# First RMSNorm of a diffusion trunk: squares summed onto all partitions by a matrix of ones, root on ScalarE, reciprocal on VectorE

## The chip, the cores and the metric

The kernel runs on one NeuronCore of a Trainium2 chip. The metric is the device time of one execution in microseconds (us). The engines are TensorE (PE; its weight loads are listed apart as PEld), VectorE (DVE), ScalarE (ACT), GpSimd (POOL) and SyncE (SP), which issues nearly all DMAs. Each engine works through its own instructions in order and waits for the others by semaphores.

## The reference, cut to what matters

The reference is a trunk of two layers over 256 latent and 256 context tokens of 1024 channels. Each layer starts with an RMSNorm whose result is scaled and shifted by values computed from two conditioning vectors, and multiplies it with one wide projection:

```python
def rmsnorm(x, g):
    xf = x.astype(jnp.float32)
    y = xf * lax.rsqrt(jnp.mean(xf * xf, axis=-1, keepdims=True) + EPS)
    return (y * g.astype(jnp.float32)).astype(x.dtype)
...
def modulate(h, shift, scale):
    return h * (1 + scale) + shift
...
        mod = (s_lat @ w_ada[l] + b_ada[l])[:, None, :]
        sh1, sc1, g1, sh2, sc2, g2 = jnp.split(mod, 6, axis=-1)
...
        h = modulate(rmsnorm(x, norm1_g[l]), sh1, sc1)
        hc = modulate(rmsnorm(xc, norm1_g[l]), csh1, csc1)
        p = h @ w_in[l]
```

All of it is in float32. The rest of a layer (convolution branch, neighbourhood attention, gates, two output projections and a gated MLP) is not touched by the change.

## The kernel before, in words

Channels lie on the 128 partitions and tokens along the free axis. `x` is held as eight tiles of 128 channels by 512 tokens (256 latent, then 256 context). A float32 product is made as three products of rounded parts (`mm3`, L177 to L179; in `v_tile`, L629, the parts are told apart by `parts`): a weight unit of 128x1024 is loaded by SP (`raw`), ACT rounds it to `whi`, DVE takes the rest as `wlo`, and the activations `h` are split in the same way.

The tile framework orders each engine's instructions by a plan of its own; `tc.issue_after` and the helper `queued` (L133) tie some of them to others, and `queued` above all makes one line of the first PE instructions.

The first stage is what the change touches. In order:

- Constants are set (`one`, `mhalf`), ACT loads the table of Silu and makes `sil`, the Silu of the conditioning vectors, when `cv` has come. PE runs 14 products of `ident` with itself (`busy`, L127), which write to a bank that nothing reads.
- The loop over the eight tiles (from L521) loads `x[k]`, squares it on ACT (L525; the context half of the last on DVE, L528), adds two squares on DVE (L532) and sums over the channels on PE (`sum0`, L515): for each block of 128 tokens, the squares are the stationary operand and a column of ones the moving one, so that the sums of 512 tokens come out as four columns of `sums0`, with tokens on the partitions. `busy(3)` follows each of the first three sums. Between them stand the two halves of `ada0` (`ada_half`, L200): products of `sil` with the weights `w_ada` of the scale and shift of channel tile 0.
- `root` (L332): DVE divides by 1024 and adds EPS, POOL raises to -0.5 (L336), and PE transposes the four columns, broadcast to 128 wide, with `ident` (L341), which puts 1/rms of all tokens on all partitions in a bank `po`. ACT copies it to SBUF later (L663).
- Meanwhile `ada_rows` (ACT copy, L217) and `ada_sums` (two PE transposes L224, a DVE reduction L226, the bias L228) make scale and shift of channel tile 0, and `gain` (L285) makes (1 + scale) times the norm's weight.
- `modulated` (L347) makes `h` of channel tile k: DVE multiplies `x` by gain and 1/rms (L355), ACT adds the shift and rounds (L356), DVE keeps the rest (L357).
- The loop over k (L690) then runs the products of V (`v_tile`, L629), a part of the first convolution projection (`glu0`), and, one tile ahead, the scale and shift of tile k + 1 (`ada_now`), whose weights come as two units of 512 KB for each k into four buffers that are used in turn.

From there on PE has work without a break through both layers, up to the last norm.

Of the kernel before, what the change touches and what calls it, by code (L numbers as in the profile page):

```python
# [15 lines left out]
P = 128  # L16
# [29 lines left out]
def trunk(ctx: ExitStack, tc: tile.TileContext, xt, cvec, crow, wall, wada, params, bias_t, rope_t, out):  # L46
# [28 lines left out]
    def sl(w, i):  # L75
        return w[:, i * P : (i + 1) * P]
# [39 lines left out]
    act.activation(small([P, 1], "wb", 4), one, AF.Silu)  # L116
    mhalf = cp.tile([P, 4], F32, name="mhalf")
    dve.memset(mhalf, -0.5)
    sil = ea0.tile([P, 2 * KD + 32], F32, name="sil")
    dve.memset(sil, 0.0)  # L120
    act.activation(sil[:, : 2 * KD], cv.rearrange("p k s -> p (k s)"), AF.Silu)


    warm = psum("sc")
    def busy(n):
        for _ in range(n):
            mm = pe.matmul(sl(warm, 0), ident, ident, start=True, stop=True)  # L127
        return mm


    queue = [busy(14)]

    def queued(f, *a):  # L133
        with tc.issue_after(queue[-1].ins):
            queue.append(f(*a))
# [7 lines left out]
    def raw_unit(src, r=None):  # L143
        r = wp.tile([P, UW], F32, tag="raw", bufs=4, name=nm("raw")) if r is None else r
        lastdma[0] = sp.dma_start(r, src)
        return r
# [51 lines left out]
    def ada_half(ps, u, r):  # L198
        for g in range(4):
            mm = pe.matmul(  # L200
                ps[32 * g : 32 * g + 32, :S], sil[:, 8 * u + 2 * g : 8 * u + 2 * g + 32], r[:, g * S : (g + 1) * S],
                start=u == 0, stop=u == 1,
            )
        return mm

    def ada_products(l, j, bank, place=lambda: None):

        ps = psum(bank)
        for u in range(2):
            ada_half(ps, u, raw_unit(wada[l, 2 * j + u], place()))  # L210
        return ps

    lastev = [None]
# [1 line left out]
    def ada_rows(ps):  # L215
        ev = tmp()[:, :S]
        lastev[0] = act.copy(ev, ps[:, :S])  # L217
        return ev

    def ada_sums(l, j, ev):  # L220
        n = slice(j, j + 9, 8) if l == 0 and j < 8 else slice(2 * j, 2 * j + 2)
        pt = psum("pt")
        for i in range(2):
            mm = pe.transpose(sl(pt, i), sl(ev, i), ident)  # L224
        m = mods[l][:, n, :]
        dve.tensor_reduce(m, pt[:, :S].rearrange("p (i g s) -> p i s g", i=2, g=4)[:, :, 0:2, :], AX.X, ALU.add)  # L226
        b = par[:, l * NPAR + BADA : l * NPAR + BADA + 6 * KD][:, n].unsqueeze(2).to_broadcast([P, 2, 2])
        dve.tensor_tensor(m, m, b, ALU.add)  # L228
        return mm
# [32 lines left out]
                    tmp().bitcast(BF16), r, v, 1.0, pr(l, BADA + n, 1), ALU.mult, ALU.add, mods[l][:, n, s : s + 1]  # L262
                )

    def ada_now(j, place):
        ev = ada_rows(ada_products(0, j, "po", place))
        yield
        ada_sums(0, j, ev)
        gain(0, 1, N1G, j)
# [9 lines left out]
    def gain(l, part, off, k, ns=2):  # L279

        if (l, part) not in gains:
            gains[l, part] = cp.tile([P, KD, 2], F32, name=f"gain{l}_{part}")
        a = gains[l, part][:, k, :ns]
        g = pr(l, off + k, 1).to_broadcast([P, ns])
        dve.scalar_tensor_tensor(a, mod2(l, part, k)[:, :ns], 1.0, g, ALU.add, ALU.mult)  # L285
# [46 lines left out]
    def root(pt, nt, n, bank):  # L332
        red = small([P, nt], "red")
        mid = dve.tensor_scalar(red, pt[:, :nt], 1.0 / n, EPS, ALU.mult, ALU.add)
        rs = small([P, nt], "rs")
        pool.tensor_tensor(rs, red, mhalf[:, :nt], ALU.pow)  # L336
        yield mid
        yield
        pb = psum(bank)
        for t in range(nt):  # L340
            pe.transpose(sl(pb, t), rs[:, t : t + 1].to_broadcast([P, P]), ident)  # L341
        return pb
# [170 lines left out]
    sums0 = psum("pt")  # L513

    def sum0(q, first, last):  # L515
        for t in range(4):
            mm = pe.matmul(sums0[:, t : t + 1], sl(q, t), one, start=first and t == 0, stop=last, skip_group_check=True)
        return mm

    ada0 = psum("po")  # L520
    for k in range(KD):  # L521
        sp.dma_start(x[k], xt[k])
        q = tmp()
        if k < KD - 1:
            act.activation(q, x[k], AF.Square)  # L525
        else:
            act.activation(q[:, LAT], x[k][:, LAT], AF.Square)
            dve.tensor_tensor(q[:, CTX], x[k][:, CTX], x[k][:, CTX], ALU.mult)  # L528
        if k >= KD - 2:
            queued(sum0, q, False, k == KD - 1)  # L530
        elif k % 2:
            dve.tensor_tensor(q, q, prev, ALU.add)  # L532
            queued(sum0, q, k == 1, False)
            queued(busy, 3)
        prev = q
        if k >= KD - 3 and k != KD - 2:
            ra = raw_unit(wada[0, k // (KD - 1)])
            if k < KD - 1:
                queued(ada_half, ada0, 0, ra)
# [3 lines left out]
    for l in range(DEPTH):  # L543
# [5 lines left out]
        with ExitStack() if last else start as e1a:  # L549
# [68 lines left out]
            with ExitStack() as e1b:  # L618
# [4 lines left out]
                def v_tile(pv, w, k, toks, parts=range(3)):  # L623
                    i = k % 2
                    for t in toks:
                        c = slice(t * P, (t + 1) * P)
                        b = slice(i * 512, (i + 1) * 512)
                        for n in parts:
                            pe.matmul(  # L629
                                pv[t], h1[n == 1][k][:, c], w[n == 2][:, b], start=k + n == 0, stop=k == KD - 1 and n == 2  # L630
                            )

                if l == 0:

# [4 lines left out]
                    def place():  # L639
                        places[0] += 1  # L640
                        if places[0] % 2:
                            return eb.tile([P, UW], F32, tag="q", bufs=2, name=nm("raw"))
                        return eb.tile([P, UW], F32, tag="k", bufs=2, name=nm("raw"))

                    sums = root(sums0, 4, D, "po")
                    next(sums)
                    ev = ada_rows(ada0)
                    rv = wp.tile([P, UW], F32, tag="raw", bufs=4, name=nm("raw"))
                    wv = [wp.tile([P, UW], F32R, tag=t, bufs=4, name=nm(t)) for t in ("whi", "wlo")]
# [10 lines left out]

                    def more():
                        act.copy(wg[0][:, cuts[0]], rg[:, cuts[0]])
                        act.copy(pb, ps)  # L663
                        act.copy(wv[0][:, cuts[1]], rv[:, cuts[1]])
                        act.copy(wg[0][:, cuts[1]], rg[:, cuts[1]])
                        for w, r, c in ((wv, rv, cuts[0]), (wg, rg, cuts[0]), (wv, rv, cuts[1])):
                            low_part(w, r, c)

                    queued(busy, 2)
                    queued(ada_sums, 0, 0, ev)  # L670
                    gain(0, 1, N1G, 0)
                    with tc.issue_after(queue[-1].ins):
                        ps = whole(sums)
                        queue.append(busy(6))
                    pb = tp.tile([P, 512], F32, tag="ss", name="rstd0")
                    pg0 = [psum("sc") for _ in range(2)]

                    wgs = {0: wg}
# [11 lines left out]
                    for k in range(KD):  # L690
                        if k % 2 == 0 and k:
                            with tc.issue_after(low[0].ins), tc.issue_after(low[1].ins):
                                wv = wunit(l, U_V + k // 2, cuts=2)
                        low = modulated(0, ps if k == 0 else pb, 1, 0, k, h1, (0, 1))
                        if k == 0:
                            with tc.issue_after(low[0].ins), tc.issue_after(low[1].ins):
                                more()
                            with tc.issue_after(queue[-1].ins):
                                v_tile(pv, wv, k, range(4), parts=(0,))
                            v_tile(pv, wv, k, range(4), parts=(1,))  # L700
                        elif k == 1:
                            with tc.issue_after(low[1].ins):
                                low_part(wg, rg, cuts[1])
                        if k == 5:
                            with tc.issue_after(lastdma[0].ins):
                                sp.dma_start(par[:, DW:], params[:, DW:])
                                sp.dma_start(rope, rope_t)
                        if k + 1 < KD:
                            nxt = ada_now(k + 1, place)
                            next(nxt)  # L710
                        v_tile(pv, wv, k, range(4), parts=range(3) if k else (2,))
                        if k + 1 < KD:
                            finish(nxt)
                        glu0(2 if k else 1)
# [220 lines left out]
        with ExitStack() as e2:  # L935
# [101 lines left out]
                    ffn_out(i - 3, pss[2 * i - 6], pss[2 * i - 5])  # L1037
            if not last:
                h1 = h_tiles()
            if last:  # L1040
                eps = small([P, 1], "wb", 4)
                dve.memset(eps, EPS)
            sss = sum_squares(NS, S, last)
            NB = 0 if last else KD - 2
            if not last:
# [167 lines left out]
```

## Time and profile before

| | us |
|---|---|
| median of 3 runs | 1130.89 |
| lowest and highest run | 1130.51, 1132.48 |
| span of the profiled execution, first to last instruction | 1127.4 |
| PE busy in the span | 1115.5 |
| DVE busy | 906.5 |
| ACT busy | 565.7 |
| first product of the V projection (L629) | at 18.03 |

The profile gives the span of the profiled execution, which is 3.5 us under the median of the timed runs; what lies before its first and after its last instruction is not in it. A line of the profile names the line of the kernel, the engine, the operation, and the tiles as out<-in. In the timeline a line is start, duration, engine, and what was made; in the chain of waits, start and the time that it added to the chain. A float32 product of two operands is recorded as two passes, so that 14 products of `busy` stand as x28. Matmuls overlap, so that one's recorded duration is longer than the time between two of them.

### The profile page before, as it was taken

The page shows a single profiled execution, that of the slowest core. Times are in us where ns is not written, and L with a number is a line of the kernel's source. Part 1 is how long each engine was busy: PE and PEld are TensorE (multiplying, and loading weights), DVE is VectorE, ACT ScalarE, POOL GpSimd, SP SyncE. Part 2 cuts the span into 40 slices and gives each one's busy share as a digit, 9 for nine tenths or more (in the row PEclk, how much of TensorE's full clock was granted, in tenths as well). Part 3 has the DMA queues.
Part 4 walks back from the last instruction along what each step waited for, and adds up shares of the span by engine and source line. Part 5 has one row for each costly group of instructions (what it writes and reads, how often), then busy time and mean ns, then how long its engine had stood idle before and what let it go on. Part 6 is the DMA issues. An engine that isn't in the chain of part 4 may idle for free.

```text
span 1127.4 us, 17780 instructions
## 1 busy us (share of the span) xinstructions
PE 1115.5 (99%) x6854; PEld 965.1 (86%) x6854; DVE 906.5 (80%) x1625; ACT 565.7 (50%) x937; POOL 17.2 (2%) x24
## 2 busy tenths in 40 slices
PE   9999999999999999999999999999999999999997
PEld 7678777787789988888888888989898999999997
DVE  4689999786778788888898555789996898988773
ACT  4347657542334543444334223544677667766642
POOL 0000000000000000000000000010000000000000
PEclk9999999999999999999999999999999999999999
DMA  8832231635734354545556656555533575665781
GB/s 325 310 100 89 92 117 38 200 99 198 248 120 145 110 170 133 184 152 155 165 181 205 214 188 197 176 194 174 154 109 120 180 247 175 187 193 182 213 274 57
DMA packets 53941, 190.83 MB, mean 169 GB/s; under 512 B 6240, under 2 KB 6496, under 8 KB 53856
## 3 DMA queue, kind: packets, MB, share of 16 engines
q1 hardware_dynamic: 53568, 189.65, 52.6%
q8 instruction: 54, 0.88, 0.3%
q14 instruction: 31, 0.25, 0.1%
q10 hardware_dynamic: 288, 0.04, 0.0%
HBM read 188.62 MB, written 1.05 MB: 168 GB/s over the span
## 4 chain that ended last, share of the span: by engine, by line
PE 85%; DVE 10%; DMA 2%; ACT 2%; issue 1%; POOL 0%; SPq 0%; DVEq 0%; ACTq 0%; POOLq 0%
PE main L177 25%; PE main L179 24%; PE main L178 24%; DVE cb L576 4%; PE main L629 4%; DVE wlo L159 2%; DMA raw<-in_wall 1%; PE sc L127 1%; PE sc L177 1%; PE sc L179 1%; PE sc L178 1%; PE po L200 1%; PE po L502 1%; DMA sb<-in_crow 1%; PE sc L430 0%
## 5 line engine op out<-in xcount | busy, mean ns | idle before, releaser
L177 PE MATMUL main<-h,whi 128*128 128x256 f32 (+1 forms) x1328 | 446.8, 337 | 0.0
L179 PE MATMUL main<-h,wlo 128*128 128x256 f32 (+1 forms) x1328 | 443.4, 335 | 0.5 <-DVE wlo L159 0.5
L178 PE MATMUL main<-h,whi 128*128 128x256 f32 (+1 forms) x1328 | 442.4, 333 | 0.0
L158 ACT CAST whi<-raw 128x1024 fp32r<-128x1024 f32 (+1 forms) x244 | 252.5, 1039 | 284.7 <-PE main L178 128.6
L159 DVE TENSOR_TENSOR wlo<-raw,whi 128x1024 fp32r<-128x1024 f32 (+1 forms) x244 | 293.7, 1209 | 113.3 <-ACT whi L158 108.6
L177 PEld LDWEIGHTS main<-h,whi 128*128 128x128 f32 x1328 | 249.5, 188 | 32.0 <-issue 3.9
L179 PEld LDWEIGHTS main<-h,wlo 128*128 128x128 f32 x1328 | 249.5, 188 | 28.9 <-DVE wlo L159 0.7
L178 PEld LDWEIGHTS main<-h,whi 128*128 128x128 f32 x1328 | 249.9, 188 | 28.1 <-issue 0.2
L576 DVE SCALAR_TENSOR_TENSOR cb<-u,par,cb 128x512 f32<-128x512 f32 (+1 forms) x240 | 140.6, 620 | 1.2
L261 DVE CUSTOM_DVE_ANT_0 t<-raw,sb,par 128x1024 bf16<-128x1024 f32 x100 | 126.9, 1280 | 1.4 <-ACT sb L245 1.2
L177 PE MATMUL main<-fh,whi 128*128 128x256 f32 (+1 forms) x386 | 123.0, 319 | 0.0
L178 PE MATMUL main<-fl,whi 128*128 128x256 f32 (+1 forms) x386 | 122.9, 319 | 0.0
L179 PE MATMUL main<-fh,wlo 128*128 128x256 f32 (+1 forms) x386 | 122.9, 318 | 0.0
L178 PEld LDWEIGHTS main<-fl,whi 128*128 128x128 f32 x386 | 72.7, 188 | 5.6
L177 PEld LDWEIGHTS main<-fh,whi 128*128 128x128 f32 x386 | 72.7, 188 | 5.6
L179 PEld LDWEIGHTS main<-fh,wlo 128*128 128x128 f32 x386 | 72.7, 188 | 5.5
L948 ACT ACTIVATE t<-main,par 128x512 f32<-128x512 f32 (+1 forms) x82 | 50.7, 669 | 35.3 <-PE main L179 35.3
L949 DVE SCALAR_TENSOR_TENSOR t<-main,par,t 128x510 f32<-128x510 f32 (+1 forms) x82 | 47.6, 616 | 8.2 <-ACT t L948 7.6
L952 DVE SCALAR_TENSOR_TENSOR t<-main,par,t 128x510 f32<-128x510 f32 (+1 forms) x82 | 46.6, 611 | 0.0
L356 ACT ACTIVATE h<-t,mod 128x256 fp32r<-128x256 f32 x56 | 25.2, 502 | 37.5 <-DVE t L355 37.4
L883 DVE SCALAR_TENSOR_TENSOR x<-main,mod,x 128x256 f32<-128x256 f32 x48 | 22.1, 480 | 23.6 <-PE main L179 23.4
L629 PE MATMUL main<-whi,h 128*128 128x512 f32 x128 | 40.6, 402 | 0.0
(217 smaller groups left out, 1198.0 us busy)
## 6 DMA issues: line engine op xcount, KB each, us to landing
raw<-in_wall SPq DMA_DIRECT2D x239, 512.0 KB, 4.2
raw<-in_wada SPq DMA_DIRECT2D x88, 512.0 KB, 4.4
bias<-in_bias_t SPq DMA_DIRECT2D x8, 640.0 KB, 4.4
row<-in_wada SPq DMA_DIRECT2D x8, 512.0 KB, 4.8
sb<-in_crow SPq DMA_DIRECT2D x5, 512.0 KB, 6.1
x<-in_xt SPq DMA_DIRECT2D x8, 256.0 KB, 4.6
raw<-in_wall SPq DMA_DIRECT2D x8, 256.0 KB, 6.8
out<-t SPq DMA_DIRECT2D x3, 256.0 KB, 2.1
```

What stands on the lines that cost most here:

```text
L158: act.copy(hi[:, c], r[:, c])
L159: dve.tensor_tensor(lo[:, c], r[:, c], hi[:, c].bitcast(F32), ALU.subtract)
L177: pe.matmul(ps, w[0], xh, start=start, stop=False)
L178: pe.matmul(ps, w[0], xl, start=False, stop=False)
L179: pe.matmul(ps, w[1], xh, start=False, stop=stop)
L261: dve.tensor_tensor_reduce(tmp().bitcast(BF16), r, v, 1.0, pr(l, BADA + n, 1), ALU.mult, ALU.add, mods[l][:, n, s : s + 1])
L356: high = act.activation(hi[:, c], y[:, c], AF.Identity, bias=b)
L576: dve.scalar_tensor_tensor(cb[j], src, w, cb[j], ALU.mult, ALU.add)
L629: pe.matmul(pv[t], h1[n == 1][k][:, c], w[n == 2][:, b], start=k + n == 0, stop=k == KD - 1 and n == 2)
L948: act.activation(c, pv_, AF.Identity, bias=pr(l, FDB + t, 1), scale=w[1])
L949: dve.scalar_tensor_tensor(c[:, :, 1:], pv_[:, :, : S - 1], w[0], c[:, :, 1:], ALU.mult, ALU.add)
L952: dve.scalar_tensor_tensor(c[:, :, : S - 1], pv_[:, :, 1:], w[2], c[:, :, : S - 1], ALU.mult, ALU.add)
```

## The change

`sum0` becomes one product for each tile of squares, with a 128x128 matrix of ones as stationary and the 512 squares as moving operand: the sums come out on all partitions at once. ACT takes the root of sums/1024 + EPS (a new use of the Sqrt table, loaded ahead, behind `sil`), DVE the reciprocal, in place in the SBUF tile `pb`. `root` with POOL's power and the four transposes, and ACT's copy of `po`, are gone for this norm. The squares of tiles 1, 3 and 5 go to DVE. The first `busy` has 11 products, the one behind the first sum has 2, those behind the second and third sum are gone. For channel tile 0 the gain is made straight from the reduction, as sum times weight plus (1 + bias) times weight, the second made ahead, so that the bias need not be added first. The first products of `ada_now` are tied behind V's. `EPS` becomes one tile for both uses.

```diff
+    eps = cp.tile([P, 1], F32, name="eps")
+    dve.memset(eps, EPS)
...
+    act.activation(small([P, 1], "wb", 4), one, AF.Sqrt)
...
-    queue = [busy(14)]
+    queue = [busy(11)]
...
-    def ada_products(l, j, bank, place=lambda: None):
+    def ada_products(l, j, bank, place=lambda: None, after=None):
         ps = psum(bank)
         for u in range(2):
-            ada_half(ps, u, raw_unit(wada[l, 2 * j + u], place()))
+            r = raw_unit(wada[l, 2 * j + u], place())
+            with tc.issue_after(after.ins) if after else ExitStack():
+                ada_half(ps, u, r)
...
         m = mods[l][:, n, :]
+        if (l, j) == (0, 0):
+            g, first = pr(0, N1G, 1), small([P, 1], "wb", 4)
+            dve.scalar_tensor_tensor(first, pr(0, BADA + KD, 1), 1.0, g, ALU.add, ALU.mult)
         dve.tensor_reduce(m, pt[:, :S].rearrange("p (i g s) -> p i s g", i=2, g=4)[:, :, 0:2, :], AX.X, ALU.add)
+        if (l, j) == (0, 0):
+            gains[0, 1] = cp.tile([P, KD, 2], F32, name="gain0_1")
+            dve.scalar_tensor_tensor(gains[0, 1][:, 0, :], mod2(0, 1, 0), g, first.to_broadcast([P, 2]), ALU.mult, ALU.add)
...
     def sum0(q, first, last):
-        for t in range(4):
-            mm = pe.matmul(sums0[:, t : t + 1], sl(q, t), one, start=first and t == 0, stop=last, skip_group_check=True)
-        return mm
+        return pe.matmul(sums0, one.to_broadcast([P, P]), q, start=first, stop=last)
...
-        if k < KD - 1:
-            act.activation(q, x[k], AF.Square)
-        else:
+        if k == KD - 1:
             act.activation(q[:, LAT], x[k][:, LAT], AF.Square)
             dve.tensor_tensor(q[:, CTX], x[k][:, CTX], x[k][:, CTX], ALU.mult)
+        elif k % 2:
+            dve.tensor_tensor(q, x[k], x[k], ALU.mult)
+        else:
+            act.activation(q, x[k], AF.Square)
...
             queued(sum0, q, k == 1, False)
-            queued(busy, 3)
+            if k == 1:
+                queued(busy, 2)
...
-                    sums = root(sums0, 4, D, "po")
-                    next(sums)
+                    pb = tp.tile([P, 512], F32, tag="ss", name="rstd0")
+                    act.activation(pb, sums0, AF.Sqrt, bias=eps, scale=1.0 / D)
+                    dve.reciprocal(pb, pb)
...
-                        act.copy(pb, ps)
...
-                    gain(0, 1, N1G, 0)
-                    with tc.issue_after(queue[-1].ins):
-                        ps = whole(sums)
-                        queue.append(busy(6))
-                    pb = tp.tile([P, 512], F32, tag="ss", name="rstd0")
+                    queued(busy, 6)
...
-                        low = modulated(0, ps if k == 0 else pb, 1, 0, k, h1, (0, 1))
+                        low = modulated(0, pb, 1, 0, k, h1, (0, 1))
...
-                            nxt = ada_now(k + 1, place)
+                            nxt = ada_now(k + 1, place, None if k else vmm)
```

The order on the engines that follows from it differs from the old one in the first stage and hardly anywhere else. On SP the second half of V's unit for k = 4 is issued ahead of the `w_ada` units of k = 3, and the rest of the parameters (352 KB) ahead of those of k = 5. On ACT and DVE one rounding and one subtraction for a later weight unit change places with a neighbour, late in that loop.

More of the change, by code (lines that the diff above doesn't have):

```diff
@@ L263, in ada_dots, with ada_now @@
                 )
-    def ada_now(j, place):
-        ev = ada_rows(ada_products(0, j, "po", place))
+    def ada_now(j, place, after):
+        ev = ada_rows(ada_products(0, j, "po", place, after))
         yield
@@ L628, in v_tile @@
                         for n in parts:
-                            pe.matmul(
+                            mm = pe.matmul(
                                 pv[t], h1[n == 1][k][:, c], w[n == 2][:, b], start=k + n == 0, stop=k == KD - 1 and n == 2
                             )
+                    return mm
                 if l == 0:
@@ L699, in trunk @@
                                 v_tile(pv, wv, k, range(4), parts=(0,))
-                            v_tile(pv, wv, k, range(4), parts=(1,))
+                            vmm = v_tile(pv, wv, k, range(4), parts=(1,))
                         elif k == 1:
@@ L1039, in trunk @@
                 h1 = h_tiles()
-            if last:
-                eps = small([P, 1], "wb", 4)
-                dve.memset(eps, EPS)
             sss = sum_squares(NS, S, last)
```

## The prediction

> **What bounds the kernel now.** The page's head first: one engine is never idle.
>
> ```profile
> span 1127.4 us, 17780 instructions
> PE 1115.5 (99%) x6854; PEld 965.1 (86%) x6854; DVE 906.5 (80%) x1625; ACT 565.7 (50%) x937; POOL 17.2 (2%) x24
> ```
>
> PE is busy for 1115.5 us of 1127.4, but the mean says nothing about the stage that changes. So next the busy time by stage: the first 18 us, and the V projection behind them (columns: stretch, its length, then for PE, PEld, DVE, ACT and POOL busy us and instructions, granted clock, DMA share, GB/s).
>
> ```profile
> 18.00:62.00 44.00, 43.98 (x272) 30.75 (x272) 27.47 (x65) 20.29 (x41) 0.00 (x0) 1.00 0.76 275
> ```
>
> Behind 18 us PE has no gap, so whatever lets that stage begin earlier lets it end earlier, as long as the transfers keep up. What sets its beginning is read from the chain of waits (start, time added):
>
> ```profile
> 1.83 5.78 PE sc L127 x28
> ...
> 8.40 0.78 PE sc L127 x6
> ...
> 10.74 0.79 PE pt L517 x8
> 11.53 0.78 PE sc L127 x6
> 12.30 0.57 PE po L200 x8
> 12.87 1.88 PE pt L517 x16
> 14.75 0.57 PE po L200 x8
> 15.31 0.64 PE sc L127 x4
> ...
> 16.76 1.34 PE sc L127 x12
> 18.10 2.05 PE main L629 x8
> 20.15 1.00 PE po L200 x16
> ```
>
> It is PE's own queue: filler products (L127), the sums (L517) and the first conditioning products (L200) stand one behind the other, and the sums over tiles 6 and 7 begin at 12.87 only because the fillers of 11.53 and a conditioning half stand ahead. Had their inputs come by then? The start of ACT and DVE in the timeline:
>
> ```profile
> 1.65 1.28 ACT L116 ACT_TABLE_LOAD   x1 [1.65 <-PEq L1202]
> ...
> 3.82 0.21 ACT L121 ACTIVATE sil<-cv 128x16 f32<-128x16 f32 x1 [0.67 <-DMA cv<-in_cvec]
> ...
> 5.94 2.69 ACT L525 ACTIVATE t<-x 128x512 f32<-128x512 f32 x4 [0.86 <-DMA x<-in_xt]
> ...
> 10.14 0.63 ACT L525 ACTIVATE t<-x 128x512 f32<-128x512 f32 x1 [1.51 <-DMA x<-in_xt]
> ...
> 10.83 0.43 DVE L528 TENSOR_TENSOR t<-x 128x256 f32<-128x256 f32 x1 [1.48 <-DMA x<-in_xt]
> ```
>
> Tile 6 is squared by 10.77 and tile 7 by 11.26: about 2 us of the chain is PE's queue, not data. From the sums to the first V product:
>
> ```profile
> 15.38 0.37 ACT L217 COPY t<-po 128x256 f32<-128x256 f32 x1 [4.15 <-PE po L200]
> ...
> 16.28 0.17 DVE L226 TENSOR_REDUCE mod<-pt 128x4 f32<-128x16 f32 x1 [1.33 <-PE pt L224]
> ...
> 16.69 0.16 DVE L285 SCALAR_TENSOR_TENSOR gain<-mod,par 128x2 f32<-128x2 f32 x1
> 16.95 0.87 DVE L355 SCALAR_TENSOR_TENSOR t<-x,gain,po 128x256 f32<-128x256 f32 x2
> 17.47 0.91 ACT L356 ACTIVATE h<-t,mod 128x256 fp32r<-128x256 f32 x2 [1.20 <-DVE t L355]
> 18.03 2.12 PE L629 MATMUL main<-whi,h 128*128 128x512 f32 x8
> ```
>
> L355 at 16.95 needs the gain (made at 16.69 from the second conditioning half) and 1/rms. The V products follow 1.08 us later. The start of L355 is the quantity to forecast.
>
> **The change part by part.** The prices of the new operations, from the nearest rows: a product with a matrix of ones (chain of waits at the layer norm), ACT from PSUM with pointers and without, DVE by one source and by two, and the reciprocals there are.
>
> ```profile
> 229.19 0.86 PE po L832 x2
> ...
> L948 ACT ACTIVATE t<-main,par 128x512 f32<-128x512 f32 x42 | 30.4, 774 | 35.3 <-PE main L179 35.3
> L591 ACT ACTIVATE t<-main 128x512 f32<-128x512 f32 x3 | 1.8, 597 | 0.0
> ...
> L574 DVE TENSOR_SCALAR cb<-u,par 128x512 f32<-128x512 f32 x4 | 2.2, 546 | 0.0
> L532 DVE TENSOR_TENSOR t<-t,t 128x512 f32<-128x512 f32 x3 | 2.1, 693 | 6.3 <-ACT t L525 6.3
> ...
> L453 DVE RECIPROCAL ri<-sm x32: 151/158/173, 89.4 to 857.8; 128x1 f32<-128x1 f32 x32
> L469 DVE RECIPROCAL ri<-sm x8: 156/159/171, 121.3 to 191.8; 128x2 f32<-128x2 f32 x8
> ```
>
> *Sums.* One costs 0.86 us where four narrow products cost 0.79: five of them lose 0.35 us of PE. In return the fillers lose 3 + 1 + 3 + 3 products.
>
> *Table and squares.* The Sqrt table load stands behind `sil`, at 4.03. As L116 it takes 1.28 and its trial 0.20, so tile 0 is squared at about 5.45 to 6.08, not at 3.95. DVE has squared tile 1 by then (0.69), adds by 6.80, and PE's 11 fillers end there too: 28 passes took 5.78 with the last 6 at 0.13 each, so the slow ones took 0.227, and 1.83 + 22 x 0.227 = 6.82. First sum 6.83 to 7.69, two fillers to 8.14. DVE squares and adds tile 3 by 8.12 (two times 0.69 from 6.72), tile 5 by 9.44. The sums run at 8.17 and 9.50, the second to 10.36.
>
> The Trainium skill ("ScalarE: Activation LUTs", What ACT_TABLE_LOAD costs) charges 2.66 us for every switch of set, 1.28 of load and 1.38 of drain. This trace has the load at 1.28 and no such drain: L116's activation follows at 2.95.
>
> *Tail.* Conditioning half 0 (0.57) from 10.36 to 10.93; its weights were issued ahead of tile 6, which ACT took at 10.14. Sums of tiles 6 and 7: 10.93 + 2 x 0.86 = 12.65. Half 1 then runs from 12.65 to 13.29 (recorded 0.64 from its start). Its weights came at 5.2 + 6.8 = 12.0:
>
> ```profile
> L145 SPq DMA_DIRECT2D raw<-in_wada x1: 708/708/708, 5.2 to 5.2; - x1
> ...
> DMA to landing us min/median/max: 6.8/6.8/6.8
> ```
>
> *Root.* The last pass ends at 12.81. Sqrt from PSUM with one pointer lies between 0.60 (L591) and 0.77 (L948); I take 0.69, ending 13.54. ACT's copy of the conditioning rows waits behind it, at about 13.45 instead of 15.38: 1.93 earlier, and the transposes and the reduction L226 with it, at 14.35. `more` loses one ACT copy, and POOL's power and four transposes go; none of that was the last to arrive, so I count nothing.
>
> *Reciprocal.* It runs from 13.58 and delays nothing until it takes more than 0.77, when it holds up L226 on DVE's queue. No trace row is wider than two elements. From below it is the 0.55 of L574. From above the rows bound it badly: the medians grow by 1 ns for the second element, the lowest of one to the median of two by 8 ns (0.16 + 510 x 0.008 = 4.2 us), the lowest of one to the highest of two by 20 ns (10.4). I take 0.67, by the medians, near the rows L574 and L532.
>
> The Trainium skill speaks against it: "VectorE: DVE Perf Modes" (First, the fixed hardware budget) has reciprocal as an iterated divide with a repeat count of 8. If that means eight cycles for an element, 512 would take an estimated 4.3 us, and L355 would start later than today. The medians above, one ns apart, do not show it; no row here is wide enough to exclude it.
>
> *Gain in one step.* The bias addition leaves the way: L226 to L285 was two steps of 0.2, now one, and the addition follows in DVE's shadow. Worth 0.18, between nothing and 0.21. Its second factor, made ahead from `par`, costs 0.16 where DVE waits for ACT anyway.
>
> *Transfers.* The V stage starts 2.1 earlier, its weights do not:
>
> ```profile
> L145 SPq DMA_DIRECT2D raw<-in_wada x1: 328/328/328, 9.4 to 9.4; - x1
> ...
> DMA to landing us min/median/max: 9.0/9.0/9.0
> ```
>
> The second unit for k = 1 lands at 18.4. Its half would be wanted at 20.15 + 0.50 - 2.1 = 18.55: just enough. This caps the gain near 2.25. Units of k = 3 and later are issued when PE frees their buffers, and so come earlier with it; on SP, 256 KB of V's unit now go ahead of k = 3 and 352 KB of parameters ahead of k = 5, 0.9 to 1.3 us at 275 GB/s. If that were not covered by the stage's idle quarter of DMA time (share 0.76), it would cost up to 1.3 once; I count nothing.
>
> *Sum:* 1.93 + 0.18 = 2.1 us off the start of L355, and off the end, as PE follows without a gap: span 1127.4 - 2.1 = 1125.3. The median lies 3.5 above that span: **1128.8**.
>
> **The rivals.**
>
> *A slow reciprocal (slower).* For: it is the one new operation that no row prices, and L226, the gain and the first L355 all queue behind it on DVE. Against: the medians. L355 starts 0.49 after L226, so it breaks even with today's 16.95 when the reciprocal ends at 16.46, after 2.9 us (5.3 ns an element). At 4.2 us: L226 at 17.8, L355 at 18.3, 1.3 later, **1132.2**; past 5.1 us the loss is over 2.26; at 10.4, 1138.3. Read as eight cycles, that page's rule ends near 1132 too.
>
> *Weights late.* If the unit of 18.4 lands 0.5 later, or those behind it on SP's changed order do, PE stands again: gain 1.6, **1129.3**. For: the DMAs are full until then; against: their order is unchanged up to that unit.
>
> *First squares late.* If the second table switch waits as long again as it loads (1.28 more), the tile 0 square, both additions and the sums slide; the third sum then ends at 11.6, the tail 1.3 later, gain 0.8: **1130.1**. Against: L591's activations and L116's show none. This is the time by that page on ACT tables, too.
>
> **How the numbers follow.** Forecast 0.68, slow reciprocal 0.22, late weights 0.06, late squares 0.04. About 0.2% (2.26 us) is what a measurement of this kernel can tell from no change: under 1128.6 is faster, over 1133.2 slower. The forecast's own range is 1127.8 to 1129.9, by Sqrt's bounds, the gain's, and the runs' spread of 2 us. The line of 1128.6 cuts it near the middle; the freed ACT copy and transposes, counted at nothing, can only add: 0.40 faster, 0.28 same. The slow reciprocal is 0.13 slower (from 5.1 to 10.4 us is the wider stretch of its bounds) and 0.09 same; the other two are same. Faster 0.40, same 0.47, slower 0.13. Range 1127.8 to 1132.8: it takes in the slow reciprocal at 4.2 us and leaves out its far end (some 0.14) and a little below.
>
> **What would show it.** L355's first start at 14.8, V's first product at 15.9; sums of tiles 6 and 7 done at 12.8; Sqrt 0.69; the reciprocal 0.67. Wrong if the reciprocal is over 0.8, if the sums of the first tiles are PE's wait, if PE waits at the conditioning products of k = 1 for more than 0.3, or if the gap to today's V products is not kept until 62 us.

## The result and the profile after

| | before | after |
|---|---|---|
| median of the runs, us | 1130.73 (15 runs, 1128.81 to 1134.64) | 1133.16 (15 runs, 1131.73 to 1136.08) |
| ratio after to before, 95% interval | | 1.0023, 1.0014 to 1.0033 |
| span of the profiled execution, us | 1127.4 | 1131.3 |
| first product of V at (us) | 18.03 | 18.82 |
| PE busy in the span (us) | 1115.5 | 1114.0 |

The change makes the kernel slower by 0.23% (some 2.6 us). The forecast was 1128.8, and the range's upper end of 1132.8 does not hold the median. The chain of waits after, over the stage of the change (start, time added, what):

```profile
4.04 1.28 ACT L124
...
5.54 0.53 ACT t L539
...
9.63 1.12 PE pt L527 x2
...
11.33 1.93 PE pt L527 x4
...
13.28 0.70 ACT rstd L659
...
14.00 3.35 DVE rstd L660
...
17.41 0.23 DVE gain L237
...
18.82 3.47 PE main L641 x8
22.29 1.00 PE po L203 x16
```

Before, this chain was PE's own queue from 1.83 us on. Now ACT and DVE carry it to the third sum at 9.63, PE to 13.25, and then it goes through one DVE instruction of 3.35 us, the reciprocal (L660). The timeline shows what stands behind it (start, duration, engine, what, idle time before and its releaser):

```profile
14.00 3.35 DVE L660 RECIPROCAL rstd<-rstd 128x512 f32<-128x512 f32 x1 [2.85 <-ACT rstd L659]
...
14.30 0.44 PE L229 MATMUL pt<-ident,t 128*128 128x128 f32 x2
...
14.58 1.50 PE L130 MATMUL sc<-ident 128*128 128x128 f32 x12
17.27 0.11 DVE L234 TENSOR_REDUCE mod<-pt 128x4 f32<-128x16 f32 x1
...
17.75 0.87 DVE L366 SCALAR_TENSOR_TENSOR t<-x,gain,rstd 128x256 f32<-128x256 f32 x2
...
18.82 3.47 PE L641 MATMUL main<-whi,h 128*128 128x512 f32 x8 [2.74 <-ACT h L367]
```

The transposes that L234 reduces are done at 14.74, but L234 stands behind the reciprocal in DVE's queue until 17.27. PE runs its six fillers to 16.08 and stands idle for 2.74 us. And the eight V products then take 3.47 us where they took 2.05 before. Why is seen in the table by stretches (columns as in the prediction; the granted clock stands behind POOL's busy time):

```profile
14.97:18.38 3.41, 1.11 (x10) 0.92 (x9) 3.34 (x6) 0.12 (x1) 0.00 (x0) 1.00 1.02 416
18.38:21.80 3.42, 2.98 (x7) 2.40 (x8) 2.93 (x6) 2.34 (x5) 0.00 (x0) 0.50 0.85 322
```

From 18.38 to 21.80 the clock of PE is granted at half. In the 3.41 us ahead of it PE was busy for only 1.11. This is one execution; e7, below, is another of the same kernel, without the half clock. In the chains, V's first eight products begin at 18.10 before and 18.82 after, and the conditioning products behind them at 20.15 and 22.29: of these 2.14 us, 0.72 is the later start and 1.42 the clock.

The two spans differ by 3.9, not 2.14. The rest lies far behind the change: held against the same DVE instructions of before, after is 2.2 us late at 62 us, 1.5 at 900 and 3.7 at 945. From 900 to 945 layer 1's output projection waits for weights. PE's busy time (third number) there, before and after:

```profile
900.00:945.00 45.00, 44.02 (x367) 43.51 (x367) 41.74 (x80) 29.36 (x54) 0.70 (x1) 1.00 0.71 238
```

```profile
900.00:945.00 45.00, 41.79 (x350) 41.38 (x349) 39.84 (x76) 28.42 (x48) 0.70 (x1) 1.00 0.74 245
```

PE stands 0.98 us there before and 3.21 after. All engines have their instructions there in the same order in both kernels, and e5 to e7 show how far this stretch differs between executions of one kernel.

### The profile page after: what moved, and what is told of

Its sections match the earlier page's. It is cut to its first block, busy times and chain, and to the rows that moved or that the text cites. A ratio compares the mean times of both kernels' runs of the same rounds, so it can differ in the third digit from the quotient of the medians.

```text
span 1131.3 us, 17671 instructions
## 1 busy us (share of the span) xinstructions
PE 1114.0 (98%) x6800; PEld 960.0 (85%) x6800; DVE 911.0 (81%) x1629; ACT 565.1 (50%) x936; POOL 13.8 (1%) x23
## 4 chain that ended last, share of the span: by engine, by line
PE 85%; DVE 10%; DMA 2%; ACT 2%; issue 1%; DVEq 0%; SPq 0%; ACTq 0%
PE main L180 25%; PE main L182 24%; PE main L181 24%; DVE cb L588 4%; PE main L641 4%; DVE wlo L162 2%; DMA raw<-in_wall 1%; PE sc L180 1%; PE sc L182 1%; PE sc L181 1%; PE po L203 1%; PE po L513 1%; DMA sb<-in_crow 1%; PE sc L441 0%; PE sc L495 0%
```

## The experiments

The theory after this result: the loss is the width of the reciprocal, and PE's standing still behind it costs a stretch of half clock on top. The rivals: the wide sums, the table loads and the new order cost it; or the later stage does. The line numbers in each profile are those of its own kernel. All diffs are against the changed kernel, except where another is named.

| kernel | first V product at, profile | half clock up to 1100 us, profile | mean clock of the runs | median us (runs) | ratio to before, 95% interval |
|---|---|---|---|---|---|
| before | 18.03 | none | 0.9951 (92) | 1130.73 (15) | 1 |
| e5, before again | 21.60 | 14.83 to 21.66, 939.85 to 943.26 | | 1134.87 (1) | |
| e6, before again | 21.60 | 14.65 to 21.48 | | 1132.88 (1) | |
| after | 18.82 | 18.38 to 21.80 | 0.9950 | 1133.16 (15) | 1.0023, 1.0014 to 1.0033 |
| e7, after again | 18.97 | none | | 1131.22 (1) | |
| e1 no reciprocal | 16.41 | 933.49 to 936.90 | 0.9965 | 1129.45 (12) | 0.9979, 0.9966 to 0.9992 |
| e2 18 fillers | 18.76 | 740.35 to 743.76 | 0.9961 | 1133.32 (12) | 1.0006, 0.9993 to 1.0019 |
| e3 pieces | 18.97 | 935.60 to 942.43 | | 1134.39 (1) | |
| e4 four columns | 20.81 | 9.22 to 19.46, 937.64 to 944.47 | 0.9920 | 1132.80 (12) | 1.0007, 0.9993 to 1.0021 |
| e8 four columns, filled | 19.61 | 12.59 to 19.42 | 0.9946 | 1131.11 (12) | 1.0000, 0.9987 to 1.0013 |
| e9 two turns | 16.95 | none | 0.9962 | 1131.86 (12) | 0.9994, 0.9981 to 1.0008 |
| e10 before, fewer fillers | 20.93 | 9.24 to 19.48, 937.66 to 941.08 | 0.9935 | 1133.21 (12) | 1.0017, 1.0008 to 1.0027 |
| e11 two turns, none ahead | 17.51 | 935.77 to 939.18 | 0.9966 | 1130.92 (12) | 0.9991, 0.9978 to 1.0003 |
| e12 Ln and Exp | 17.67 | 937.25 to 940.66 | 0.9960 | 1132.15 (12) | 1.0003, 0.9988 to 1.0018 |

The mean clock is the granted clock averaged over an execution and then over the timed runs (for before, over 92 runs in the comparisons of e1 to e12). One step of 3.41 us at half takes 0.0015 from it, about 1.7 us. The median of before was 1130.73 in the first comparison, 1131.92 in that of e1 to e4, then 1131.63, 1131.75 and 1131.66; so kernels of different comparisons are set against each other by their ratios.

**e1: no reciprocal.** A multiplication by one stands in its place, so 1/rms is left out.

```diff
-                    dve.reciprocal(pb, pb)
+                    dve.tensor_scalar(pb, pb, 1.0, 0.0, ALU.mult, ALU.add)
```

> Leaves out the reciprocal: one DVE multiplication by 1.0 of the same 128x512 tile stands in its place. Theory A (the loss is the reciprocal's 3.35 us on DVE's queue, and the half clock that follows from PE's idle time behind it): the operation takes 0.55 to 0.7 us, the first L366 starts at 15.0 to 15.2, the first V product at 16.1 to 16.3, the eight V products take 2.05 us again and no half clock stands between 18 and 22 us; the time is 1.6 to 2.1 us under before, 4 to 4.5 under the changed kernel. Theory B (the loss comes from what else changed: fewer fillers, squares shared with DVE, the order on SP, the tie of the conditioning products): the time stays at or over before even without the reciprocal.

The timeline of e1, DVE:

```profile
14.01 0.43 DVE L660 TENSOR_SCALAR rstd<-rstd 128x512 f32<-128x512 f32 x1 [3.04 <-ACT rstd L659]
14.79 0.17 DVE L234 TENSOR_REDUCE mod<-pt 128x4 f32<-128x16 f32 x1 [0.35 <-PE pt L229]
...
15.34 0.88 DVE L366 SCALAR_TENSOR_TENSOR t<-x,gain,rstd 128x256 f32<-128x256 f32 x2
```

L234 now waits for PE's transposes and no longer for DVE. L366 starts at 15.34, V at 16.41 (each some 0.1 later than expected), the clock stays full in this stage, and the ratio falls from 1.0023 to 0.9979, the intervals apart. All else in the change was kept, wide sums, table loads and order: they do not make the loss.

**e2: 18 fillers.** PE is kept at work while DVE inverts.

```diff
-                    queued(busy, 6)
+                    queued(busy, 18)
```

> The changed kernel with 18 filler products in place of 6 while the reciprocal runs, which keeps PE at work until about 18.6 us. Theory A: the granted clock stays full, the first eight V products take 2.05 instead of 3.47 us, the first still starts at 18.8; the time is 1.3 to 1.7 us under the changed kernel, about 0.7 to 1.0 over before. Theory B, with the clock independent of PE's idle time there: the drop stays and the time is that of the changed kernel.

The table by stretches of e2, and its chain:

```profile
14.97:18.38 3.41, 3.41 (x33) 3.41 (x32) 3.34 (x6) 0.18 (x1) 0.00 (x0) 1.00 1.03 418
18.38:21.80 3.42, 3.36 (x28) 1.96 (x27) 2.87 (x6) 2.28 (x5) 0.00 (x0) 1.00 0.74 277
```

```profile
13.93 3.35 DVE rstd L660
...
18.76 2.10 PE main L641 x8
```

The reciprocal is as long and V starts as late, but with PE at work the clock stays full and the eight products take 2.10. One profile doesn't show that the fillers did this, since e3 and e7 kept the clock without them. The timed runs speak for it: their mean clock is 0.9961 against 0.9950 for the change, some 1.2 us. In the time it isn't shown: the ratio is 1.0006, between that of e1 and that of the change, and its interval overlaps that of the change. By the three ratios the half clock is worth 0.17% (1.9 us; 1.42 in the profile that has it) and the reciprocal 0.27% (3.1 us; V's start 2.35 earlier). By the medians, each less that of before beside it, they are 1.0 and 3.9 us. The intervals are about 0.13% either way, so the split is rough.

**e3: the reciprocal cut into 256, 128, 64 and 64 columns**, to see what sets its price.

```diff
-                    dve.reciprocal(pb, pb)
+                    for lo_, hi_ in ((0, 256), (256, 384), (384, 448), (448, 512)):
+                        dve.reciprocal(pb[:, lo_:hi_], pb[:, lo_:hi_])
```

> The reciprocal cut into pieces of 256, 128, 64 and 64 columns. If an element costs 6.4 ns and the instruction some 0.1 us, they take about 1.7, 0.9, 0.5 and 0.5 us. If instead the 3.35 us are a price of the instruction (a wait, another program on DVE), the pieces take as long each or their sum is far from 3.35 plus three small fixed prices.

The view of that one line (count, then lowest, median and highest ns):

```profile
L661 DVE RECIPROCAL rstd<-rstd x4: 495/695/1753, 14.1 to 17.0; 128x64 f32<-128x64 f32 x2, 128x256 f32<-128x256 f32 x1, 128x128 f32<-128x128 f32 x1
```

The lowest is a piece of 64, the highest that of 256: (1753 - 495) / 192 = 6.6 ns for an element. From 256 to the whole 512 it is (3352 - 1753) / 256 = 6.2 ns. The price goes with the width, with little besides. The one timed run says nothing by itself.

**e4 and e8: four columns.** The narrow sums are put back, with tokens on the partitions; Sqrt and reciprocal work on 128x4, and PE transposes the four columns onto all partitions, as `root` did. e4 keeps the change's fillers (11 and 2), e8 has 14, 3 and 3, those of before but for the last three.

```diff
-        return pe.matmul(sums0, one.to_broadcast([P, P]), q, start=first, stop=last)
+        for t in range(4):
+            mm = pe.matmul(sums0[:, t : t + 1], sl(q, t), one, start=first and t == 0, stop=last, skip_group_check=True)
+        return mm
...
-                    dve.reciprocal(pb, pb)
+                    std, rs = small([P, 4], "red"), small([P, 4], "rs")
+                    act.activation(std, sums0[:, :4], AF.Sqrt, bias=eps, scale=1.0 / D)
+                    dve.reciprocal(rs, std)
...
+                            mm = pe.transpose(sl(ps, t), rs[:, t : t + 1].to_broadcast([P, P]), ident)
...
-    queue = [busy(11)]
+    queue = [busy(14)]
...
-            if k == 1:
-                queued(busy, 2)
+            if k < 5:
+                queued(busy, 3)
```

(The last two pieces are e8's alone.)

> The changed kernel, but with the sums as four columns again (tokens on the partitions), Sqrt and reciprocal of 128x4, and four PE transposes to spread them; table load, shared squares, fewer fillers, one-step gain and tied conditioning products as in the change. Theory A: the reciprocal takes 0.16 to 0.2 us, the first L366 starts at 14.6 to 15.0, the time is 1.9 to 2.4 us under before. Theory B: as slow as before or slower.

> As with four columns before (Sqrt and reciprocal of 128x4, four transposes), but with 14 fillers first and 3 behind each of the first two sums, so that PE has no gaps up to the third sum. Theory C: in the run with fewer fillers the clock fell to half from 9.2 to 19.5 us because PE did little; with the fillers it stays full once it is, the first L366 starts at 14.8 to 15.6, and the time is 1.0 to 2.0 us under before. Rival: the narrow sums hold no clock, fillers or not; the clock falls again, and the time is that of the run with fewer fillers.

DVE's timeline in e4, and the stretches of e4 by clock:

```profile
16.47 0.18 DVE L662 RECIPROCAL rs<-red 128x4 f32<-128x4 f32 x1 [5.34 <-ACT red L661]
```

```profile
5.80:9.22 3.42, 2.90 (x26) 2.71 (x24) 2.80 (x5) 1.53 (x3) 0.00 (x0) 1.00 1.02 380
9.22:19.46 10.24, 9.96 (x53) 8.23 (x53) 1.32 (x5) 2.20 (x5) 0.00 (x0) 0.50 1.02 407
```

The reciprocal costs 0.18, as theory A had it, and yet V starts at 20.81: from 9.22 on, PE runs for three stretches of 3.41 us at half clock, though the profile has it busy for 9.96 of 10.24. With more fillers (e8) it is two such stretches, 12.59 to 19.42, V starts at 19.61, and the time is that of before. So both theories missed: A had left out the clock, and C's fillers did not hold it. A small reciprocal alone is no gain here: what it saves on DVE, the narrow sums lose on PE.

**e5, e6, e7: before, twice, and after, once more, unchanged**, since the base of the prediction was one execution.

> The kernel before, unchanged, for another profile. Theory C: the granted clock becomes full at a moment that differs from run to run (6.87 us in the first profile of before, 4.73 in that of the changed kernel), and PE's chain of fillers and sums in the kernel before is the longer the later that is: with the clock full at 4.7 us the first V product starts near 17.0, at 8.1 near 18.7. Theory D: it starts at 18.0 to 18.1 whatever the clock does, and what the changed kernel loses beyond its later start is lost in a stage behind 62 us.

> The same once more, for a second moment of the clock. Theory C: the first V product starts earlier where the clock is full earlier, about 0.5 us for each us. Theory D: 18.0 to 18.1.

> The changed kernel, unchanged, for another profile. The reciprocal takes 3.35 us again and the first V product starts at 18.6 to 19.2 whatever the clock does before (the sums of tiles 6 and 7 wait for data). Theory C: whether a half clock falls on the V products depends on where the clock's windows of 3.41 us lie against PE's idle 2.7 us; so it may be missing here, and the eight products then take 2.05 us.

The chain of waits of e5, to be held beside that of before, and its stretches:

```profile
13.41 2.18 PE pt L517 x16
15.60 1.01 PE po L200 x8
...
19.04 2.56 PE sc L127 x12
21.60 1.93 PE main L629 x8
```

```profile
8.00:14.83 6.83, 6.83 (x65) 6.30 (x64) 1.12 (x2) 1.25 (x3) 0.00 (x0) 1.00 1.03 404
14.83:21.66 6.83, 6.83 (x36) 6.01 (x36) 3.06 (x10) 2.96 (x7) 1.02 (x1) 0.50 0.85 330
```

The unchanged kernel has the half clock too, in both of these executions (in e6 from 14.65 to 21.48), and V starts at 21.60 in both, not at 18.03. Neither theory had that: the clock first became full at 8.01 and 7.83, for which C asked for 18.7 at most. Alike up to here, the two differ by 2.0 us in span (1133.1 and 1131.1), and e5 has one more step at half clock far behind, which shows as 0.96 in the stretch from 900 us, e6 none:

```profile
900.00:945.00 45.00, 42.89 (x346) 42.48 (x345) 39.21 (x72) 27.37 (x45) 0.69 (x1) 0.96 0.74 245
```

```profile
900.00:945.00 45.00, 43.02 (x360) 42.61 (x359) 41.26 (x78) 28.53 (x48) 0.70 (x1) 1.00 0.73 245
```

e7 is the change without the half clock: V at 18.97, and these stretches, where PE's 2.74 us of standing are spread over two:

```profile
14.20:17.61 3.41, 2.03 (x18) 1.80 (x16) 3.38 (x3) 0.71 (x2) 0.00 (x0) 1.00 1.03 422
17.61:21.02 3.41, 2.05 (x8) 1.41 (x9) 3.20 (x9) 2.46 (x5) 0.00 (x0) 1.00 1.03 401
```

Busy for 2.03 and 2.05 of 3.41 the clock held; busy for 1.11 it was halved. e3, whose four pieces take 3.39 together, stands idle as long and held it too, busy for 2.20 and 1.85 in the two steps. So one of three profiles with the long reciprocal and six fillers has the half clock. By these, which of the two comes depends on where the steps of the clock fall, and that differs between executions: it first became full at 4.73 us in after and at 7.38 in e7. A sharp limit they don't give: busy for 1.99 in the step from 932.36 of e11, PE was at half clock in the next, and busy for 1.65 in the step from 933.16 of after it was not.

**e9, e11: two turns.** From the changed kernel: the wide sums and the wide Sqrt stay, PE transposes the four blocks of roots so that each token stands on a partition, DVE inverts 128x4, PE transposes the columns back.

```diff
-                    dve.reciprocal(pb, pb)
+                    pt4, ps, rs = psum("sc"), psum("po"), small([P, 4], "rs")
...
+                            mm = pe.transpose(sl(pt4, t), sl(pb, t), ident)
...
+                            mm = pe.transpose(sl(ps, t), rs[:, t : t + 1].to_broadcast([P, P]), ident)
...
                     queued(busy, 2)
+                    queued(turn)
+                    dve.reciprocal(rs, pt4.rearrange("p (t c) -> p t c", t=4)[:, :, 0])
                     queued(ada_sums, 0, 0, ev)
-                    queued(busy, 6)
+                    queued(spread)
+                    queued(busy, 4)
```

What `turn` writes is inverted from its first column of each block, and the bank `po` takes the place of `pb` for channel tile 0. e11 leaves out the `busy(2)` ahead of `turn` and has `busy(6)` behind `spread`.

> Computes the reference. From the changed kernel: the wide sums and the Sqrt over 128x512 stay; PE transposes the four blocks of 128 roots, so that each token's root stands on a partition, DVE inverts 128x4, PE transposes the four columns back onto all partitions. Theory (the loss is the width of the reciprocal and PE's idling behind it; wide sums hold the clock): Sqrt ends near 14.0, first turn by 14.6, reciprocal 0.18 by 14.9, second turn by 15.5, L366's successor at 15.4 to 15.8, first V product at 16.5 to 16.9, no half clock there; 1.4 to 2.3 us under the kernel before (e1, without any reciprocal, was 2.4 under it). Rival (the two turns on PE and their hand-overs cost as much as the wide reciprocal): first V product at 18 or later, time within 0.7 us of the kernel before.

> Computes the reference. The kernel of e9 without the two fillers in front of the first turn (they held it from 13.99, the end of Sqrt, to 14.47) and with six instead of four behind the second turn. Theory (each 0.1 us that the start of the V products gains stays in the time, and e9's missing gain is the spread of the runs): first turn at 14.05, reciprocal 0.18 by 14.7, second turn by 15.5, L366's successor at 15.45 (e9: 15.87), first V product at 16.5 (16.95); 1 to 2 us under the kernel before. Rival (a gain at the start is given back at the weight waits between 900 and 935 us, whatever the start): first V product at 16.5 too, but the time within 0.6 us of the kernel before.

The chain of waits of e9, then of e11:

```profile
13.83 0.64 PE sc L130 x4
14.47 0.45 PE sc L664 x4
...
14.95 0.19 DVE rs L696
...
15.19 0.66 PE po L669 x4
...
15.87 0.49 DVE t L366
...
16.95 2.10 PE main L641 x8
```

```profile
13.85 0.70 ACT std L659
...
14.59 0.67 PE sc L664 x4
...
16.17 1.34 PE sc L130 x12
17.51 1.88 PE main L641 x8
```

From the end of Sqrt to L366 it takes 1.88 us in e9 (13.99 to 15.87) where it took 3.78 with the wide reciprocal (13.97 to 17.75). In e9 the steps came up to 0.35 us later than in the theory, V at 16.95 for 16.9; the time moved less than expected: ratios of 0.9994 and 0.9991, whose intervals both hold 1 and both lie below that of the change. In e11 the turn follows Sqrt at once, but Sqrt itself came 0.55 later than in e9 (its chain has a tile of `x` that landed only at 8.64), and the two fillers added at the end reached to 17.51, the start of V, where 16.5 had been expected. So the two turns give back what the change lost; that they beat before isn't shown.

**e10: before with fewer fillers.** The diff is against the kernel before.

```diff
-    queue = [busy(14)]
+    queue = [busy(11)]
...
-            queued(busy, 3)
+            if k == 1:
+                queued(busy, 2)
```

> Computes the reference. The kernel before with its fillers cut as in the change (14, 3, 3, 3 to 11, 2, 0, 0) and nothing else. By the prediction's reading that PE's queue sets the chain (2 us between the squares and the last sums) the sums of tiles 6 and 7 are done near 12.9 instead of 14.75 and L355 starts at about 15.3 to 15.6, 1.3 to 1.6 us under the kernel before. By the clock's theory (narrow sums don't hold it, so that fillers do) the clock drops to half between 9 and 20, the V products begin no earlier than 18.5 and the time is 0 to 3 us above the kernel before.

The chain of waits of e10:

```profile
12.64 3.50 PE pt L517 x16
...
20.93 1.87 PE main L630 x8
```

Ten fillers fewer, and the sums of tiles 6 and 7 end 1.4 us later than in before's first profile (16.14 against 14.75): 16 narrow products take 3.50 instead of 1.88, at half clock from 9.24 to 19.48. The ratio is 1.0017, 1.0008 to 1.0027, and the mean clock 0.9935 against 0.9951. The fillers of before hold the clock, if not always; they are no slack.

**e12: Ln and Exp.** ACT makes 1/rms alone.

```diff
-    act.activation(small([P, 1], "wb", 4), one, AF.Sqrt)
+    act.activation(small([P, 1], "wb", 4), one, AF.Ln)
...
-                    act.activation(pb, sums0, AF.Sqrt, bias=eps, scale=1.0 / D)
-                    dve.reciprocal(pb, pb)
+                    act.activation(pb, sums0, AF.Ln, bias=eps, scale=1.0 / D)
...
+                    with tc.issue_after(lastev[0].ins):
+                        act.activation(pb, pb, AF.Exp, scale=-0.5)
```

> Computes the reference in another form: from the changed kernel, ScalarE takes Ln of the mean square plus EPS in place of Sqrt and Exp of -0.5 times that in place of VectorE's reciprocal, with a table load between the two. Theory (the changed kernel's loss is the 3.35 us that the reciprocal of 512 elements for each partition holds VectorE): load 1.28 and Exp 0.6 to 0.7 behind the copy of the conditioning rows that ends at 14.25, so 1/rms at 16.2 instead of 17.35, L366 at 16.3 to 16.5 instead of 17.75, first V product at 17.4 to 17.6 instead of 18.82; 1.0 to 1.5 us under the changed kernel's median of the first session, 1133.16, about equal to the kernel before. Rival (what costs is the wide form itself, that PE stands idle between the sums and the V products, however long): the time stays at 1133, as with 18 fillers in e2.

The chain of waits of e12:

```profile
13.65 0.69 ACT rstd L659
...
14.64 1.28 ACT L662
...
15.93 0.64 ACT rstd L662
...
16.59 0.50 DVE t L366
...
17.67 2.12 PE main L641 x8
```

The copy of the conditioning rows, a table load and a second activation take 2.24 us (14.33 to 16.57) in place of 3.35 and leave DVE free. The ratio is 1.0003, some 2.3 us under the change and more than the 1.0 to 1.5 expected: V starts 1.15 earlier, and the mean clock is 0.0010 higher, 1.1 us. Its interval still overlaps that of the change.

## Why the prediction was wrong

*The step that failed* is the term "I take 0.67, by the medians". The reciprocal took 3.35. The medians of one and two elements, 158 and 159 ns, are a fixed price with next to nothing of the slope in it: at 6.2 ns for an element the second should have added 6, and their spread of some 20 ns hid that. The upper bound made from the same rows (4.2) was the nearer one. To choose L574 and L532 as neighbours was to take the reciprocal for an operation of the usual price, for which no row spoke. Without the mis-sized term the forecast's direction comes out: e1, with 0.43 in its place, is 0.21% (2.4 us) under before, where 2.1 was forecast. That the sizes agree so well is in part luck: V starts 1.62 earlier than in before's first profile, not 2.1, and the mean clock of e1's runs is higher by 0.0014, 1.6 us, which no step of the forecast had.

*The rival "A slow reciprocal"* had the mechanism, L234 behind it on DVE's queue, and the break-even of 2.9 us. At 3.35 its formula gives 0.45 later, about 1131.3; L366 came 0.80 later (17.75 against 16.95), since Sqrt ended 0.43 late. The Trainium skill's rule that it leaned on ("VectorE: DVE Perf Modes", First, the fixed hardware budget: an iterated divide with a repeat count of 8) pointed the right way. The prediction's estimate from it, 4.3 us, is above the 3.35 measured.

*What no branch had* is the clock. The V products were moved as a block of 2.05 us, whatever came ahead of them. The fillers were counted as time on PE only, and not for what they do to the clock: in the profile of after, PE's idle time behind a late L366 halved it for 3.41 us, 1.42 more on the path, though not in e3 and e7. The Trainium skill ("TensorE: Matmul & The Clock Gate", Part 1: The HAM clock gate) has a free-running window of some 3.4 us after whose idleness the clock is halved; the traces agree with the step of 3.41. Its rule of thumb there, no idle gap over about 3.4 us, is too mild for this case: a gap of 2.74 was enough in after, where 2.30 of it lay in one step, which had work for 1.11, and not in e7, where it lay in two.

*The base.* "1127.4 - 2.1" took one execution for the kernel. Before's other two profiles have spans of 1133.1 and 1131.1 with V at 21.60. In the 92 timed runs of before the mean granted clock goes with the time: 0.997 to 0.998 in 19 runs of 1129.5 us on average, 0.995 to 0.996 in 42 of 1131.4, 0.993 to 0.994 in 31 of 1133.9. The first profile was of the first kind. "PE's queue, not data" was right for the chain, but a queue cut short (e10) lost more by the clock than it saved.

Of the signs of being wrong, two came: the reciprocal over 0.8, and PE waiting at the first sums (0.92 us at the first, 0.27 at the third, which starts 0.13 late). The gap to before's V products was kept until 62 us: 2.14 at the conditioning products, 2.2 there.

*What held.* The table load at 4.04 for 1.28 (4.03 forecast), with the next activation at 5.34, so that the drain of 1.38 that the Trainium skill has there ("ScalarE: Activation LUTs", What ACT_TABLE_LOAD costs) does not show; the square of tile 0 at 5.54 in the chain (5.45), the second and third sum at 8.24 and 9.63 (8.17, 9.50), Sqrt 0.69, its end at 13.97 (13.54). The tail was 0.43 late: the third sum came 0.13 late, and the two passes of one wide sum took 1.12 or 0.97 instead of 0.86. The gain in one step was worth what it was given: L366 0.48 behind L234 (17.27 to 17.75; 0.49 forecast). "Weights late" and "First squares late" did not come: the chain after has no transfer in it between 9.63 and 31 us. The changed order on SP left no wait there.

*What stays open.* That the wide reciprocal makes the loss is shown by e1, and its removal in e9, e11 and e12 agrees; how the 2.6 us over before are made up is not settled. The clock doesn't make them on average: the mean clock is 0.9950 in the runs of the change and 0.9951 in those of before, so that before loses as many steps; where, the mean doesn't tell. e7, with no step at half clock, has V 0.94 later than before's first profile, with none either, and a span 2.0 longer.

Most of that comes from one unchanged stretch. Held against the same DVE instructions of before's first profile, e7 is 0.9 us late at 62 us, 0.7 at 900 and 2.1 at 945; e1 is 1.6 early, 2.2 early and 0.7 late; e9 is 1.1 early, 0.5 early and level; e4 is 2.7, 1.8 and 7.0 late. So a difference at the start lasts until 900 us to within 1.2 us (but for e2, with its half clock at 740), and the next 45 us, where PE waits for weights and half of the profiles have a half clock, add from 0.5 to 5.2 us to it. In e9 they, and a wait for conditioning rows near 210 us (1.8 us against 1.1), take back the whole gain; for that one profile the rival of e11 holds. Whether an earlier start makes the waits there longer, or before's first profile was a lucky one (PE stood 0.98 us there, and 2.11 and 1.98 in e5 and e6), no run tells.

## What to carry to other kernels

A price that grows with the width can't be read from rows of width one and two: where no wide row exists, take the pessimistic bound as the case to plan for, or shrink the operand (one value for each token is 128x4; the same values on all partitions are 128x512). Work that "only fills" may hold the clock: before cutting it, look at how much of each step of the clock PE is busy, and with products of what shape. And take a second profile of the kernel before, before a change of 2 us is reckoned from the first.

## What the runs showed of the hardware

- The reciprocal of VectorE, float32 on 128 partitions: 0.16 us for one column, 0.18 for 4 (e4, e9), 0.495 for 64, 1.75 for 256, 3.35 for 512: 6.2 to 6.6 ns for a column. A multiplication of the same 512 in place took 0.43 (e1).
- The granted clock of TensorE changed only in steps of 3.41 us (18.38 to 21.80 in after; two steps from 14.83 to 21.66 in e5; three from 9.22 to 19.46 in e4), and their phase differs between executions.
- PE may be busy by the profile and still lose the clock. In e5 it was busy for 6.83 of 6.83 us ahead of the drop, with sums whose moving operand is one column wide and fillers between them; in e4 and e10, with fewer fillers, the clock fell earlier and stayed down for longer. With the sums 512 columns wide (after, e1, e2, e3, e7, e9, e11, e12) the only drop in the first 22 us is that of after, behind PE's idle time. That the narrow products count for little is a reading that fits all of these, with before's first profile as the one that kept the clock in spite of them; a kernel with nothing but the one or the other was not run.
- An activation follows a table load within 0.02 us in after, and within 0.01 in e12, with the load 1.28 each time.
